# Three quarters of an expert's slots as lanes beside streamed weights, and GpSimd without the experts' low parts

## Chip, cores and metric

The kernel runs on one core of a Trainium2 chip. The metric is the device time of one execution in microseconds; a kernel's time is the median of its runs.

## What is computed

A trunk of two layers runs over 256 tokens (and 16 prepended ones). Each layer has a gated linear recurrence and a convolution, then a channel mixer. The second layer's mixer is a mixture of eight experts, and almost half of the time is spent on it:

```python
def moe_swiglu(x, w_router, w_gate, w_up, w_down):
    t = x.reshape(B * L, D)
    logits = (t @ w_router).astype(jnp.float32)
    top_val, top_idx = lax.top_k(logits, TOP_K)          # 2 of 8
    top_w = jax.nn.softmax(top_val, axis=-1)
    ...
    for e in range(N_EXPERTS):
        out = out + gates[:, e:e + 1] * swiglu(t, w_gate[e], w_up[e], w_down[e])
```

`swiglu(x)` is `(silu(x @ w_gate) * (x @ w_up)) @ w_down`. A token has 1024 channels, an expert 3584 hidden columns, and all of it is float32.

## The kernel before

**Precision.** TensorE takes float32 in a rounded form (float32r), so each float32 operand is split into a high part and a low part. A product is then three products: high by high, low by high, high by low. ScalarE (ACT) copies the high part of a piece of weights (`whi`, line 116), and another engine subtracts it from the raw piece to get the low part (`wlo`): VectorE (DVE, line 94) for most pieces, GpSimd (POOL, line 218) for those that `lo_pool` (line 315) names. Of the experts' 672 pieces, those with `i % 4 == 1` are GpSimd's, but for the last ones.

**Weights.** A piece is 1024 floats on each of 128 partitions (512 KB). SyncE's queue loads it (`load_ahead`, line 269, DMA issue on line 279) as soon as one of six `raw` buffers is free; a buffer is free when the low part has been made from it. Six `whi` and six `wlo` buffers hold split pieces, and a split buffer is free when TensorE has used it. `prep` (line 282) splits pieces in order, up to five ahead of the products. All engines work through their instructions in the order in which the program recorded them.

**Experts.** Tokens are gathered to slots by products with a one-hot matrix. The experts are sorted by their numbers of tokens into positions, except for position 0, which is fixed. Positions 0, 2 and 3 are *narrow*: 128 slots. Positions 4 to 7 are *slim*: 64 slots, where the array holds the 64 slots' high parts and their low parts side by side as 128 columns, so that two products (by `whi`, by `wlo`) give everything; `fold_parts` (line 576) adds the two halves with small products against a folding matrix. Position 1, the expert with the most tokens, is *wide*: 256 slots.

An *item* is gate, up or down for 512 of the hidden columns of one position; it takes four pieces of weights. Narrow and slim items hold the tokens in the array and stream 512 columns of weights past them: 24 products of 512 columns for a narrow item, 16 for a slim one. The wide gate and up items are turned round: the array holds 128x128 of the weights, and 256 slots stream past (lines 1497 to 1499), 96 products of 256 columns for an item. A wide down item has 48 products of 512 columns (lines 1481 to 1483), two tiles of 128 slots by three products.

**Order.** `moe_seq` (line 1337) makes positions 0, 2, 3 first (21 groups of gate, up, down), then positions 4, 5, 6 with one item of position 1 after each of their 21 groups (`WIDE`, line 53), then position 7 alone. A *round* below is one slim group and one wide item, 16 pieces. What evacuates a product is put on a list (`pend`, `pend2`) and recorded while the next item is under way: for a wide up item that is `times` (line 1544), which multiplies silu(gate) by up for 1024 floats and splits the result; for slim items `fold_parts`; for wide down items `gain` (line 1520), which adds a group's result to a sum.

**Overflow.** Tokens beyond a position's slots are handled after the main sequence, in a branch (`moe_rest`, line 1735) that runs only if there are any.

Of the kernel before, what the change touches and what calls it, by code (L numbers as in the profile page):

```python
# [42 lines left out]
# The product after which a block's evacuation comes; pieces to be ready after pairs of rows; the order of the  # L43
# parts (of the weights, of x) where several blocks are made at once.
# [4 lines left out]
# Experts by position: the first one is fixed, the others are sorted. Wide items after each group, the items before  # L49
# which a gather begins, the groups by which the last position's down products wait.  # L50
# [6 lines left out]
# Columns at which the engines share the rows of tokens, and products that keep the tensor engine's clock up.  # L57
# [11 lines left out]
class Halves:  # L69
    """A [128, 8, n] tensor kept as two tiles of four blocks."""  # L70
# [9 lines left out]
class Priced:  # L80
    """The vector engine, with an estimate of how long it has been given work for."""
# [17 lines left out]
class Tables:  # L99
    """The scalar engine; the functions are taken from three table sets."""  # L100
# [18 lines left out]
class Trunk:  # L119
# [101 lines left out]
    def plan(self):  # L221
# [3 lines left out]
        def piece(w, a, b, c0):  # L225
            """Up to four blocks of rows of a unit's columns."""
# [129 lines left out]
    def gemm_both(self, x, n, evacs, other, before=None):  # L356
        """Two units against all of n tokens, block of rows by block of rows, as x comes."""
# [34 lines left out]
    def level_bits(self):  # L392
        """The bits in which s and t differ, of t after s."""
# [95 lines left out]
    def rstd_col(self, mv, k):  # L489
        """mv[:, 1] holds a variance; returns 1 / sqrt(var + eps)."""  # L490
# [6 lines left out]
    def tok_mean(self, t, k, between=None):  # L497
        """[mean, variance] of the rows of t."""
# [23 lines left out]
    def input_norm(self, first):  # L522
        """The normalised tokens, transposed: returns their two parts and the work that makes a block."""
# [22 lines left out]
        def block(b):  # L546
            """The low part of a block waits until the next block is under way."""
# [17 lines left out]
    def norm_sums(self, s, r, first, eng=None):  # L565
        """Add a block to the sums of r and of r * r over the blocks."""
# [16 lines left out]
    def rstd(self, mu, e2, n):  # L583
        """1 / sqrt(e2 - mu * mu + eps)."""
# [16 lines left out]
    def post_norm(self, r, s, g, b):  # L601
        """h = LN(r) * g + b, in two float32r parts; the sums in s have all blocks but the last."""
# [45 lines left out]
    def residual(self, r, h, i):  # L648
        """r block i = ALPHA * h."""
# [3 lines left out]
    def add_to(self, r, ps, b, s):  # L653
        """A block of products added to r, and its part in the sums."""
# [51 lines left out]
    def forget(self, l, j, f, k):  # L706
        """f = lb + (1 - lb) sigmoid(z) and k = (1 - lb) sigmoid(-z); lb is zero in the first layer."""
# [11 lines left out]
    def values(self, i, ps, j):  # L719
        """The value projection of a head, copied out; its transposes come a block later."""  # L720
# [20 lines left out]
    def attention(self, hf, f, k, q):  # L741
        """Attention weights of four heads: att[s, t] = sum_d q[t] f[s + 1] ... f[t] k[s], s <= t.
        A level joins neighbouring runs of h tokens: q has the decay from its run's start, k the decay to its
        run's end, and the last of a run's f is the decay of the whole run. A mask keeps the pairs of tokens
        that a level is for; that of runs of one takes a token with itself along."""
# [47 lines left out]
        def join(h):  # L793
            """Runs of h tokens become runs of 2 h."""
# [64 lines left out]
    def heads(self, l, sog, o, t0, n):  # L859
        """o = RMS norm of att^T v per head, times the gate (the norm's gain is in it)."""  # L860
# [194 lines left out]
    def spread_rows(self, *names):  # L1055
        """Rows of parameters, put on all partitions by products."""
# [16 lines left out]
    def router_weights(self):  # L1073
        """LN(r) @ W = rstd * (r @ (g W) - mean * sum(g W)) + sum(b W), sums over d: g W and the two sums."""
# [17 lines left out]
    def residual_tok(self, h, res):  # L1092
        """ALPHA * h of the last 256 tokens, tokens on the partitions."""
# [12 lines left out]
    def out_proj1(self, mx, res):  # L1106
        """r = res + mx @ w_out with tokens on the partitions, LN(r), and the router's logits, which are taken
# [766 lines left out]
```

## Time and profile before

| | |
|---|---|
| time, median of 3 runs | 2014.54 us (2013.33 to 2029.12) |
| span of the profiled execution | 2016.8 us |
| busy in it: PE, PEld | 95%, 85% |
| busy in it: DVE, ACT, POOL | 78%, 62%, 46% |
| read from HBM | 481.73 MB, 239 GB/s over the span |

The profiled execution is 2.3 us above the median. Shares over the whole span mix stages with different limits, so the tables below are cut into stretches: the first two layers up to about 930 us, then the experts. An idle engine costs nothing unless the engine that sets the pace waits for it. Busy time of PE is modelled, and consecutive products overlap, so a product's cost is read from the distance between the starts of two, not from its duration.

### The profile page before, as it was taken

To read this page: it belongs to the slowest core of one execution; us is meant where nothing else is said; L and a number is where in the kernel's file an instruction comes from. 1 tells how busy PE (TensorE), PEld (TensorE's weight loads), DVE (VectorE), ACT (ScalarE), POOL (GpSimd) and SP (SyncE) were. 2 spreads that over 40 slices of the span, in tenths; PEclk is the share of its full clock that TensorE was granted. 3 is DMA by queue.
4 is the path that set the end of the run, shared out by engine and by line. 5 is a ranking of instruction groups with operands and counts; after the bars stand their busy time and mean duration, and the time that the engine had idled before them with its cause. 6 is when DMAs were issued, how large, how long until landed. Compare 5 with 4: busy or idle time off the path is not lost. (4 is left out here: it accounts for less than half of the span.)

```text
span 2016.8 us, 33666 instructions
## 1 busy us (share of the span) xinstructions
PE 1911.1 (95%) x12193; PEld 1719.1 (85%) x12193; DVE 1571.7 (78%) x1931; ACT 1256.5 (62%) x1707; POOL 930.5 (46%) x424
## 2 busy tenths in 40 slices
PE   9999998999999998998999999999999999999896
PEld 8999898999999998997778888887888887877664
DVE  7998628755568985378999888878878788788887
ACT  5445454544465444645767787777776766766775
POOL 6776756200078567624444444434443433434343
PEclk9999999999999999998999999999999999999998
DMA  6634344565555343564998999998998888999896
GB/s 199 186 116 136 116 128 135 158 176 166 171 157 166 115 126 115 157 204 156 353 335 299 351 358 350 355 334 304 324 317 311 311 312 304 323 316 316 296 344 221
DMA packets 284182, 485.08 MB, mean 241 GB/s; under 512 B 15042, under 2 KB 139842, under 8 KB 284006
## 3 DMA queue, kind: packets, MB, share of 16 engines
q1 hardware_dynamic: 283654, 481.75, 70.7%
q8 instruction: 97, 1.59, 0.3%
q0 software_dynamic: 320, 1.08, 0.1%
q14 instruction: 79, 0.65, 0.1%
q10 hardware_dynamic: 32, 0.01, 0.0%
HBM read 481.73 MB, written 1.05 MB: 239 GB/s over the span
## 5 line engine op out<-in xcount | busy, mean ns | idle before, releaser
L218 POOL TENSOR_TENSOR wlo<-raw,whi 128x1024 fp32r<-128x1024 f32 (+1 forms) x339 | 865.5, 2562 | 1011.4 <-ACT whi L116 970.4
L116 ACT ACTIVATE whi<-raw 128x1024 fp32r<-128x1024 f32 (+1 forms) x919 | 950.4, 1051 | 292.9 <-DMA raw<-in_moe_w_gate_dram 53.6
L94 DVE TENSOR_TENSOR wlo<-raw,whi 128x1024 fp32r<-128x1024 f32 (+1 forms) x578 | 829.9, 1476 | 192.4 <-ACT whi L116 188.1
L343 PE MATMUL mm<-h_hi,whi 128*128 128x272 f32 (+1 forms) x1280 | 378.5, 296 | 1.0 <-ACT tmp L116 1.0
L345 PE MATMUL mm<-h_hi,wlo 128*128 128x272 f32 (+1 forms) x1280 | 371.4, 290 | 0.0
L344 PE MATMUL mm<-h_lo,whi 128*128 128x272 f32 (+1 forms) x1280 | 370.1, 289 | 0.0
L343 PEld LDWEIGHTS mm<-h_hi,whi 128*128 128x128 f32 x1280 | 244.8, 191 | 2.6 <-ACT tmp L116 1.2
L344 PEld LDWEIGHTS mm<-h_lo,whi 128*128 128x128 f32 x1280 | 244.9, 191 | 0.1
L345 PEld LDWEIGHTS mm<-h_hi,wlo 128*128 128x128 f32 x1280 | 244.4, 191 | 0.0
L94 DVE SCALAR_TENSOR_TENSOR st<-wide,cw,st 128x272 f32<-128x272 f32 (+1 forms) x480 | 194.4, 487 | 0.0
L1490 PE MATMUL mm<-wlo,xg 128*128 128x512 f32 x448 | 180.3, 403 | 6.1 <-DVE wlo L94 3.9
L1489 PE MATMUL mm<-whi,xg 128*128 128x512 f32 x448 | 179.0, 400 | 0.0
L1503 PE MATMUL mm<-wlo,xg 128*128 128x512 f32 x336 | 131.8, 392 | 1.4 <-DVE wlo L94 1.3
L1501 PE MATMUL mm<-whi,xg 128*128 128x512 f32 x336 | 132.4, 394 | 0.0
L1502 PE MATMUL mm<-whi,xg 128*128 128x512 f32 x336 | 131.5, 391 | 0.0
L1497 PE MATMUL mm<-xg,whi 128*128 128x256 f32 x448 | 127.6, 285 | 0.0
L1499 PE MATMUL mm<-xg,wlo 128*128 128x256 f32 x448 | 126.8, 283 | 0.0
L1498 PE MATMUL mm<-xg,whi 128*128 128x256 f32 x448 | 126.7, 283 | 0.0
L1477 PE MATMUL st<-wlo,tmp 128*128 128x512 f32 x224 | 96.2, 429 | 22.8 <-DVE wlo L94 11.5
L1490 PEld LDWEIGHTS mm<-wlo,xg 128*128 128x128 f32 x448 | 86.0, 192 | 32.6 <-DVE wlo L94 11.3
L1489 PEld LDWEIGHTS mm<-whi,xg 128*128 128x128 f32 x448 | 86.2, 192 | 19.1 <-issue 0.8
L1476 PE MATMUL st<-whi,tmp 128*128 128x512 f32 x224 | 91.0, 406 | 1.6 <-DVE tmp L94 1.6
(368 smaller groups left out, 3461.8 us busy)
## 6 DMA issues: line engine op xcount, KB each, us to landing
raw<-in_moe_w_gate_dram SPq DMA_DIRECT2D x224, 512.0 KB, 5.2
raw<-in_moe_w_up_dram SPq DMA_DIRECT2D x224, 512.0 KB, 5.8
raw<-in_moe_w_down_dram SPq DMA_DIRECT2D x224, 512.0 KB, 5.1
raw<-in_w_in_dram SPq DMA_DIRECT2D x128, 512.0 KB, 3.8
raw<-in_ffn_w_gate_dram SPq DMA_DIRECT2D x22, 512.0 KB, 4.0
raw<-in_ffn_w_up_dram SPq DMA_DIRECT2D x22, 512.0 KB, 3.9
raw<-in_ffn_w_down_dram SPq DMA_DIRECT2D x20, 512.0 KB, 3.6
raw<-in_w_conv_out_dram SPq DMA_DIRECT2D x16, 512.0 KB, 3.4
```

Source lines behind the costliest of these rows:

```text
L94: return f(out, *a, **k)
L116: return self.eng.activation(out, in_, func, **k)
L218: (eng or self.V).tensor_tensor(lo, src, f32(hi), op=ALU.subtract)
L343: nc.tensor.matmul(ps[c], w[i][0][:, a], xh, start=first, stop=False)
L344: nc.tensor.matmul(ps[c], w[i][0][:, a], xl, start=False, stop=False)
L345: nc.tensor.matmul(ps[c], w[i][1][:, a], xh, start=False, stop=last)
L1489: nc.tensor.matmul(banks[0], x(2 * h + i), whi, start=first, stop=False)
L1490: nc.tensor.matmul(banks[0], x(2 * h + i), wlo, start=False, stop=last)
L1497: nc.tensor.matmul(dst, whi[:, cc], a, start=first, stop=False, skip_group_check=True)
L1501: nc.tensor.matmul(banks[0], a, whi, start=first, stop=False)
L1502: nc.tensor.matmul(banks[0], b, whi, start=False, stop=False)
L1503: nc.tensor.matmul(banks[0], a, wlo, start=False, stop=last)
```

## The change

Position 1 gets 192 slots in place of 256, as two lanes that stand in the array at the same time as separate stationary operands: 128 slots as a narrow position has them, and 64 more as a slim position has them (`SECOND`). All its items then stream 512 columns of weights past the slots, as other positions' items do: for each block of weights three products by `whi` (narrow lane high, narrow lane low, slim lane) and two by `wlo`. A wide item becomes 40 products of 512 columns. The narrow lane's hidden values are transposed on TensorE as for narrow positions, the slim lane's are folded as for slim ones. Position 1 gets its own overflow branch for tokens beyond 192. And `lo_pool` names only two of the experts' pieces, so VectorE makes the low parts of the other 166 that GpSimd made.

```diff
+FULL, SECOND = CAP + SLIM, "second"
...
     def lo_pool(self, i):
         if i >= DENSE:
-            return DENSE + 4 <= i < DENSE + 6 or i % 4 == 1 and i < PIECES - 4
+            return DENSE + 4 <= i < DENSE + 6
...
-        for j, (p, cap) in enumerate(((0, CAP), (2, CAP), (4, SLIM))):
+        for j, (p, cap) in enumerate(((0, CAP), (1, FULL), (2, CAP), (4, SLIM))):
...
     def moe_item(self, kind, p, g, wide, slim):
+        lanes = [(p, False), (SECOND, True)] if wide else [(p, slim)]
...
+                for i, (whi, wlo) in enumerate([(whi, wlo), *more]):
+                    high, low = [], []
+                    for (q, thin), d in zip(lanes, banks):
+                        x, k = self.x[q][0], 2 * h + i
+                        high += [(d, x(k))] if thin else [(d, x[0](k)), (d, x[1](k))]
+                        low += [(d, x(k) if thin else x[0](k))]
+                    self.products(high, low, whi, wlo, h == 0 and i == 0, h == 3 and i == 1)
-                        if wide:
-                            dst = banks[j // 2][:, (j % 2) * CW:(j % 2 + 1) * CW]
-                            cc = slice(j * P, (j + 1) * P)
-                            first = first and j % 2 == 0
-                            nc.tensor.matmul(dst, whi[:, cc], a, start=first, stop=False, skip_group_check=True)
-                            nc.tensor.matmul(dst, whi[:, cc], b, start=False, stop=False, skip_group_check=True)
-                            nc.tensor.matmul(dst, wlo[:, cc], a, start=False, stop=last, skip_group_check=True)
...
+        for (q, thin), d in zip(lanes, banks):
+            if thin:
+                self.pend.append(lambda q=q, d=d: self.fold_parts(kind, q, g, d))
+            elif kind == "g":
+                self.pend.append(lambda q=q, d=d: self.silu(q, g, d))
+            else:
+                self.pend.append(lambda q=q, d=d: self.times(q, g, d))
...
-                           GW: lambda: self.gather([1], self.key, 2 * CAP),
+                           GW: lambda: self.gather_lanes(1, self.key),
```

On TensorE, the end of the first wide up item and the start of the slim item behind it. In the kernel before, `xg` are the 256 slots, streamed past 128 columns of `whi` and `wlo`:

```order
L1497 MATMUL mm_14588<-xg_13336,whi_14564 128x256
L1498 MATMUL mm_14588<-xg_13338,whi_14564 128x256
L1499 MATMUL mm_14588<-xg_13336,wlo_14565 128x256
L1489 MATMUL mm_14716<-whi_14574,xg_12344 128x512
L1490 MATMUL mm_14716<-wlo_14575,xg_12344 128x512
```

With the change, `xg_13338` and `xg_13339` are the narrow lane's high and low parts and `xg_13340` is the slim lane:

```order
L1553 MATMUL mm_14541<-whi_14518,xg_13338 128x512
L1553 MATMUL mm_14541<-whi_14518,xg_13339 128x512
L1553 MATMUL mm_14542<-whi_14518,xg_13340 128x512
L1556 MATMUL mm_14541<-wlo_14519,xg_13338 128x512
L1556 MATMUL mm_14542<-wlo_14519,xg_13340 128x512
L1553 MATMUL mm_14614<-whi_14528,xg_12345 128x512
L1556 MATMUL mm_14614<-wlo_14529,xg_12345 128x512
```

Three rows that stood four times for a block of weights have become five rows that stand once. Behind the slim item, where the kernel before had no row of position 1, the change has the narrow lane's transposes and the slim lane's folding products:

```order
L1553 MATMUL mm_14614<-whi_14594,xg_12700 128x512
L1556 MATMUL mm_14614<-wlo_14595,xg_12700 128x512
L1601 MATMUL ca_14659<-ident,four_14629 128x128 x4
L1625 MATMUL ca_14664<-fold,four_14400 128x64 x4
L1625 MATMUL ca_14664<-fold,four_14629 128x64 x4
L1553 MATMUL mm_14673<-whi_14610,xg_12345 128x512
L1556 MATMUL mm_14673<-wlo_14611,xg_12345 128x512
```

These twelve small products are new on TensorE, and they wait for `four_14629`, which VectorE writes. On VectorE, the same place of the kernel before; the first two rows are a slim position's, the `four` and `fw` rows are the wide position's `times`:

```order
L1596 TENSOR_TENSOR tmp_14644<-tmp_14643,ca_14578 128x256
L94 TENSOR_TENSOR tmp_14645<-tmp_14644,tmp_14645 128x4x64
L94 TENSOR_TENSOR wlo_14653<-raw_14524,whi_14652 128x1024
L94 TENSOR_TENSOR wlo_14683<-raw_14539,whi_14682 128x1024
L94 TENSOR_TENSOR wlo_14713<-raw_14552,whi_14712 128x1024
L1549 TENSOR_TENSOR four_14731<-four_14446,mm_14587 128x512
L1549 TENSOR_TENSOR four_14731<-four_14446,mm_14588 128x512
L94 TENSOR_TENSOR wlo_14739<-raw_14572,whi_14738 128x1024
L94 TENSOR_TENSOR wlo_14749<-raw_14613,whi_14748 128x1024
L94 TENSOR_TENSOR wlo_14759<-raw_14650,whi_14758 128x1024
L94 TENSOR_TENSOR fw_14735<-four_14731,fw_14734 128x1024
```

and with the change:

```order
L97 TENSOR_TENSOR wlo_14622<-raw_14516,whi_14621 128x1024
L1594 TENSOR_TENSOR four_14629<-four_14400,mm_14541 128x512
L97 TENSOR_TENSOR wlo_14636<-raw_14526,whi_14635 128x1024
L97 TENSOR_TENSOR wlo_14646<-raw_14553,whi_14645 128x1024
L97 TENSOR_TENSOR wlo_14656<-raw_14576,whi_14655 128x1024
L97 TENSOR_TENSOR wlo_14681<-raw_14592,whi_14680 128x1024
L97 TENSOR_TENSOR fs_14631<-ca_14659,fs_14631 128x512
L1631 TENSOR_TENSOR tmp_14693<-tmp_14692,ca_14664 128x256
L97 TENSOR_TENSOR fs_14694<-tmp_14693,fs_14694 128x4x64
L97 TENSOR_TENSOR wlo_14702<-raw_14608,whi_14701 128x1024
```

Four `wlo` rows stand where three stood, and the products of 1024 floats of the wide position (two `L1549` rows and the `fw` row) have become one product of 512, one split of 512 read from PSUM, and the slim lane's two rows of 256.

## Rows read from the trace of the kernel before

**Rows 1.** The page, its first line.

```profile
span 2016.8 us, 33666 instructions
```

**Rows 2.** Stretches: us, busy PE, PEld, DVE, ACT, POOL, granted clock, DMA share, GB/s.

```profile
941.00:1056.00 115.00, 108.40 (x488) 85.60 (x487) 113.68 (x92) 82.51 (x92) 52.83 (x18) 1.00 0.88 313
1056.00:1103.00 47.00, 47.00 (x214) 38.81 (x214) 42.70 (x36) 38.31 (x43) 22.59 (x8) 1.00 0.82 294
1103.00:1304.00 201.00, 200.72 (x938) 166.76 (x937) 170.07 (x144) 157.59 (x170) 85.97 (x34) 1.00 0.98 353
1310.00:1872.00 562.00, 532.23 (x3060) 460.15 (x3060) 459.60 (x360) 394.26 (x458) 225.25 (x84) 0.98 0.90 315
1872.00:1999.00 127.00, 112.81 (x485) 80.02 (x483) 109.03 (x94) 97.96 (x121) 50.85 (x19) 0.97 0.90 319
```

**Rows 3.** Timeline of PE: start, duration, then the instruction; two wide, then slim products.

```profile
1401.04 0.28 PE L1498 MATMUL mm<-xg,whi 128*128 128x256 f32 x1
1401.16 0.28 PE L1499 MATMUL mm<-xg,wlo 128*128 128x256 f32 x1
...
1419.36 0.39 PE L1476 MATMUL st<-whi,tmp 128*128 128x512 f32 x1
1419.59 0.39 PE L1477 MATMUL st<-wlo,tmp 128*128 128x512 f32 x1
...
1424.44 1.89 PE L1590 MATMUL ca<-fold,tmp 128*128 128x64 f32 x16
1426.14 0.36 PE L1497 MATMUL mm<-xg,whi 128*128 128x256 f32 x1
```

**Rows 4.** Waits in 1310:1872: us in total, times, longest.

```profile
PEld st L1477 <- DVE wlo L94: 19.8, 23, 2.2
...
PEld st L1477 <- POOL wlo L218: 13.3, 11, 1.5
```

**Rows 5.** Waits of the DMA queue in 1310:1872.

```profile
SPq L279 <- POOL wlo L218: 166.0, 73, 3.6
```

**Rows 6.** VectorE's durations in 1310:1872, ns, least/median/most.

```profile
L94 DVE TENSOR_TENSOR wlo<-raw,whi x252: 1207/1212/3420, 1309.2 to 1866.4; 128x1024 fp32r<-128x1024 f32 x126
...
L94 DVE TENSOR_TENSOR tmp<-tmp,tmp x21: 424/1560/1742, 1334.8 to 1857.3; 128x256 fp32r<-128x256 f32 x21
```

**Rows 7.** Timelines of DVE (two rows) and POOL (two rows), one place.

```profile
1399.85 3.68 DVE L94 TENSOR_TENSOR wlo<-raw,whi 128x1024 fp32r<-128x1024 f32 x2 [0.78 <-ACT whi L116]
...
1408.81 3.48 DVE L94 TENSOR_TENSOR wlo<-raw,whi 128x1024 fp32r<-128x1024 f32 x3
...
1398.46 2.84 POOL L218 TENSOR_TENSOR wlo<-raw,whi 128x1024 fp32r<-128x1024 f32 x1 [2.75 <-ACT whi L116]
...
1413.35 2.41 POOL L218 TENSOR_TENSOR wlo<-raw,whi 128x1024 fp32r<-128x1024 f32 x1 [4.74 <-ACT whi L116]
```

**Rows 8.** Groups in 1310:1872: busy us, mean ns | idle before.

```profile
L94 DVE TENSOR_TENSOR wlo<-raw,whi 128x1024 fp32r<-128x1024 f32 x252 | 367.7, 1504 | 83.4 <-ACT whi L116 80.2 <-PE st L1476 1.9 <-PE mm L1499 0.7
...
L218 POOL TENSOR_TENSOR wlo<-raw,whi 128x1024 fp32r<-128x1024 f32 x84 | 225.2, 2682 | 337.2 <-ACT whi L116 315.4 <-PE mm L1489 7.6 <-PE mm L1498 4.8
...
L94 DVE TENSOR_TENSOR tmp<-tmp,tmp 128x256 fp32r<-128x256 f32 x21 | 27.4, 1304 | 10.2 <-ACT tmp L116 10.2
...
L94 DVE TENSOR_TENSOR fw<-four,fw 128x1024 fp32r<-128x1024 f32 x7 | 21.7, 3093 | 0.0
...
L1549 DVE TENSOR_TENSOR four<-four,mm 128x512 f32<-128x512 f32 x14 | 9.5, 682 | 0.3
```

**Rows 9.** The low parts' groups in 941:1056 (two rows), 1103:1304 and 1872:1999.

```profile
L94 DVE TENSOR_TENSOR wlo<-raw,whi 128x1024 fp32r<-128x1024 f32 x55 | 99.6, 1863 | 1.1 <-ACT whi L116 1.1
...
L218 POOL TENSOR_TENSOR wlo<-raw,whi 128x1024 fp32r<-128x1024 f32 x18 | 52.8, 2935 | 60.8 <-ACT whi L116 60.8
...
L94 DVE TENSOR_TENSOR wlo<-raw,whi 128x1024 fp32r<-128x1024 f32 x102 | 142.1, 1433 | 25.6 <-ACT whi L116 24.8
...
L94 DVE TENSOR_TENSOR wlo<-raw,whi 128x1024 fp32r<-128x1024 f32 x62 | 87.4, 1456 | 11.1 <-ACT whi L116 11.0
```

More of the change, by code (lines that the diff above doesn't have):

```diff
@@ L1450, in gather, with gather_lanes, tiles, slice_ @@
             self.tasks += todo
+    def gather_lanes(self, p, key):
+        nc = self.nc
+        xs, box = {}, {"left": KB}
+        def tiles():
+            box["oh"] = self.one_hot([p], key, 2 * CAP)
+            for part in (0, 1, SECOND):
+                xs[part] = self.hs.tile([P, KB, P], F32R, tag="hs", name=self.name("xg"))
+        def slice_(kk, part):
+            def f():
+                src, oh = self.parts[part], box["oh"]
+                pt = self.ca((P, 2, 2 * CAP))
+                for i in range(2):
+                    k = 2 * kk + i
+                    for tt in range(2):
+                        nc.tensor.matmul(pt[:, i], src[tt][:, k * P:(k + 1) * P], oh[:, tt, 0], start=tt == 0, stop=tt == 1)
+                def evac():
+                    box["left"] -= 1
+                    b = slice(2 * kk, 2 * kk + 2)
+                    a = slice(part * SLIM, (part + 1) * SLIM)
+                    for dst, v in ((xs[part][:, b], pt[:, :, :CAP]), (xs[SECOND][:, b, a], pt[:, :, CAP:FULL])):
+                        if part:
+                            self.A.activation(dst, v, AF.Copy)
+                        else:
+                            nc.vector.tensor_copy(dst, v)
+                self.pend.append(evac)
+            return f
+        self.x[p] = [[lambda k, part=part: xs[part][:, k, :] for part in range(2)], box, 0]
+        self.x[SECOND] = [lambda k: xs[SECOND][:, k, :], box, 0]
+        self.tasks += [tiles] + [slice_(kk, part) for part in range(2) for kk in range(4)]
     def moe_item(self, kind, p, g, wide, slim):
         nc = self.nc
+        lanes = [(p, False), (SECOND, True)] if wide else [(p, slim)]
         if kind == "d" and wide:
@@ L1458, in moe_item @@
             self.y[p] = [[self.st((P, 512)) for _ in range(2)]]
-        while kind == "d" and (p, g) not in self.hid:
+        while kind == "d" and any((q, g) not in self.hid for q, _ in lanes):
             self.flush()
@@ new lines, in moe_item @@
+                first, last = h == 0 and (wide or g == 0), h == 3 and (wide or g == G - 1)
+                for c in range(2):
+                    cc = slice(c * 512, (c + 1) * 512)
+                    high, low = [], []
+                    for (_, thin), y, f in zip(lanes, self.y[p], hid):
+                        high += [(y[c], f[:, h])] if thin else [(y[c], f[0][:, h]), (y[c], f[1][:, h])]
+                        low += [(y[c], f[:, h] if thin else f[0][:, h])]
+                    self.products(high, low, whi[:, cc], wlo[:, cc], first, last)
+            else:
+                for i, (whi, wlo) in enumerate([(whi, wlo), *more]):
+                    high, low = [], []
+                    for (q, thin), d in zip(lanes, banks):
[3 more added lines that the diff above has]
+                    self.products(high, low, whi, wlo, h == 0 and i == 0, h == 3 and i == 1)
@@ L1508, in moe_item, with products @@
             self.prep(self.used + SPLIT - 1)
-        if slim and kind != "d":
-            self.pend.append(lambda: self.fold_parts(kind, p, g, banks[0]))
-        elif kind == "g":
-            self.pend.append(lambda: self.silu(p, g, banks))
-        elif kind == "u":
-            self.pend.append(lambda: self.times(p, g, banks, wide))
-        elif wide:
-            self.pend.append(lambda: self.gain(p, g, self.y[p]))
-        elif g == G - 1:
-            self.pend.append(lambda: self.finish(p))
+        if kind == "d":
+            if wide:
+                self.pend.append(lambda: self.gain(p, g, self.y[p]))
+            elif g == G - 1:
+                self.pend.append(lambda: self.finish(p))
+            return
+        for (q, thin), d in zip(lanes, banks):
[3 more added lines that the diff above has]
+                self.pend.append(lambda q=q, d=d: self.silu(q, g, d))
+            else:
+                self.pend.append(lambda q=q, d=d: self.times(q, g, d))
+    def products(self, high, low, whi, wlo, first, last):
+        seen = []
+        for d, x in high:
+            self.nc.tensor.matmul(d, x, whi, start=first and not any(d is e for e in seen), stop=False)
+            seen.append(d)
+        for d, x in low:
+            self.nc.tensor.matmul(d, x, wlo, start=False, stop=last)
     def gain(self, p, g, ys):
@@ L1533, in gain, with silu, lane_tmp @@
             self.finish(p)
-    def silu(self, p, g, banks):
-        t = self.four(F32) if len(banks) == 2 else self.tmp([P, 512])
-        for i, b in enumerate(banks):
-            self.A.activation(t[:, i * 512:(i + 1) * 512], b, AF.Silu)
+    def silu(self, p, g, bank):
+        t = self.lane_tmp(p)
+        self.A.activation(t, bank, AF.Silu)
         self.sg[p] = t
+    def lane_tmp(self, p):
+        if p == SECOND:
+            t, self.shared = self.shared, None
+            return t[:, 512:]
+        if not (p == 1 and self.lanes):
+            return self.tmp([P, 512])
+        self.shared = self.four(F32)
+        return self.shared[:, :512]
@@ L1541, in four, with times, turn @@
     def four(self, dt):
         return self.mp.tile([P, D], dt, tag="four", name=self.name("four"), bufs=6)
[L1544 removed]
+    def times(self, p, g, bank):
         nc = self.nc
[L1546 to L1550 removed]
+        f = self.lane_tmp(p)
+        nc.vector.tensor_tensor(f, self.sg[p], bank, op=ALU.mult)
+        fs = self.hs.tile([P, 2, 4, P], F32R, tag="hs", name=self.name("fs"))
+        fh, fl = fs[:, 0], fs[:, 1]
+        def turn():
+            pt = self.ca((P, 4, P))
+            for i in range(4):
+                nc.tensor.transpose(pt[:, i, :], f[:, i * P:(i + 1) * P], self.ident)
@@ L1673, in moe_run @@
     def moe_run(self, seq, start, ahead=0, wide=(), slim=()):
+        self.lanes = bool(wide)
         for n, (kind, p, g) in enumerate(seq):
@@ L1746, in moe_rest @@
                     for p in ps:
-                        self.y_hs = p > 2
+                        self.y_hs = p not in (0, 2)
                         n = nc.values_load(self.count[0:1, p:p + 1], min_val=0, max_val=S)
```

81 lines of the change are left out of this document (19 added, 62 removed).

## The prediction

> **What bounds the kernel now.** I read the stretches first [rows 2]. Up to 930 us the change touches nothing; all terms lie behind. The first narrow items (941 to 1056) have VectorE busy 113.68 of 115 us: VectorE is the limit there, while the transfers run at 313 GB/s. The short stretch to 1103 has PE busy throughout, with a gather among its products. The next 201 us run at 353 GB/s with a DMA share of 0.98: the weights' transfer is the limit. From 1310 to 1872, the 21 rounds of slim and wide items, no engine is full: DMA share 0.90, PE 532 of 562, VectorE 460. A round takes 562 / 21 = 26.76 us. Position 7 alone (1872 to 1999) is at 0.90 of DMA again.
>
> Why no engine is full in the rounds is read from the timeline of PE [rows 3]. A product of 256 columns starts 0.12 us after the one before, one of 512 columns 0.23 us. So a slim group is 48 x 0.23 = 11.04 us, its folding 1.70 (1424.44 to 1426.14). A wide gate or up item is 96 x 0.12 = 11.52, a wide down item 48 x 0.23 = 11.04, 11.36 in the mean. Together 24.10 us, so 2.66 us of a round is lost. The waits say where: slim down products wait for low parts, of VectorE 19.8 us and of GpSimd 13.3 us [rows 4]. The loads run behind too: the DMA queue waited 166.0 us for raw buffers that GpSimd's subtraction still held, though most of that was spent with other loads in flight [rows 5]. At 353 GB/s [rows 2] a piece of 0.524 MB costs 1.485 us, sixteen 23.8 us. So PE's own work, 24.10, is the largest floor of a round, and buffers that come late add the rest.
>
> **The lanes.** A wide item becomes 40 products of 512 columns: 40 x 0.23 = 9.20 us in place of 11.36. The pitch should hold: every product loads its stationary operand anew already now, 3060 loads for 3060 products [rows 2]. For three items the slim lane adds one folding (1.70 us) and the narrow lane four transposes. A folding product of 64 columns is 1.70 / 16 = 0.11 us; the four transposes have 128, so between as much and twice as much each, 0.4 to 0.9 us; I take 0.9. PE's round is then 12.74 + (27.6 + 2.6) / 3 = 22.8 us, 1.3 less. On VectorE, seven times, two products of 512 floats (0.682 each [rows 8]) and a split of 1024 (3.093) give way to one product and one split of 512 (I take 0.682 for both) and the slim lane's two rows of 256 floats, 0.424 each where undisturbed [rows 6]. ACT gets a copy, a silu and a split of the slim lane more; at 394 of 562 us [rows 2], even as much for each of the seven groups as VectorE's longest split here, 3.1 us, leaves it at 19.8 us a round. The gather keeps its products and one more copy of 64 slots hides behind PE in the narrow stretch.
>
> **The low parts.** VectorE makes 166 more pieces. What one costs is not the mean of now. In the rounds the mean is 1504 ns [rows 8], but least and median are 1207 and 1212, the longest 3420 [rows 6]. The timelines show which is which [rows 7]: two pieces at 1399.85 took 3.68 us while GpSimd's piece of 1398.46 ran until 1401.30; three at 1408.81 took 3.48, in GpSimd's idle stretch before 1413.35. GpSimd's subtraction of 2682 ns [rows 8] pushes VectorE's aside. Without it I take 1.212 for each. Bounds: 1.16 (3.48 / 3) and the mean of now, 1.504. So in the rounds VectorE's work is 336 x 1.212 = 407, the slim splits 21 x 0.424 = 9, the wide position's 7 x 2.21 = 15.5, and what is left of now (459.6 - 367.7 - 27.4 - 21.7 - 9.5 = 33.3): 465 us, 22.1 a round. It hardly rises from 459.6, though it makes a third more pieces.
>
> The Trainium skill (Perfetto Trace Analysis, Optimizing Scalar/DVE Operations) says that when VectorE is saturated, giving work to ScalarE or even GpSimd may make sense. It adds that VectorE and GpSimd share a read port, so that moving work between those two might not help. The first sentence speaks against this change and would keep the 225 us on GpSimd; the trace sides with the second.
>
> **The sum.** In the rounds three floors lie close: transfers 23.8, PE 22.8, VectorE 22.1. A round cannot be under 23.8: 500 us, -62. If PE's loss of 2.66 stayed, it would be 25.5: 535 us, -27. GpSimd's share of the waits goes, but VectorE's queue is in order, and a multiply that waits for TensorE or ScalarE now holds up every low part. I take the middle, 24.6: 517 us, **-45**. In 941 to 1056, VectorE's 99.6 us for 55 pieces [rows 9] become (55 + 18) x 1.212 = 88.5, with the other 14.1 us 102.6; the bytes (313 GB/s x 115) need 102 at 353 GB/s. I take 105, **-10** (bounds 0 and -13). To 1103 PE stays full: 0. In 1103 to 1304 the transfers stay the limit; VectorE's work is 201 x 353 / 524 = 135 pieces x 1.212 = 164 and 170.07 - 142.1 [rows 2, 9] = 28 beside: 192 of 201, so 0, but 4 us later if its waits don't hide. In 1872 to 1999 there are 77 pieces: VectorE 93 + (109.03 - 87.4) = 115 us [rows 2, 9], transfers 115; I take **-3** (bounds 0 and -12). Together -58: 2016.8 [rows 1] becomes 1959. The profiled execution was 2.3 us above the median, so **1957**.
>
> **Rivals.** *The transfers alone decide.* If the buffers keep the queue fed, every stretch but the PE-bound one runs at 353 GB/s: -62 - 13 - 12 = -87, 1927. For it: the stretch at 0.98 shows it can be done with PE and VectorE busy. Against: in the rounds PE takes slim pieces every 0.92 us and wide ones every 2.3, with twelve buffers to even that out. The Trainium skill (Perfetto Trace Analysis, Engine Utilization) gives 358 GB/s as a core's full memory bandwidth; by that a round would be 23.4 us, an estimate, and the trace's 353 agrees.
> *The loss moves to VectorE's queue.* With all low parts in one queue, behind evacuations that wait for PE, the loss of a round grows from 2.66 to 4.0 and eats what PE saves: 26.8 again. Only the -10 at the start stays: 2005. For it: VectorE's lateness is already the larger wait [rows 4]. Against: its work per round stays where it was.
> *VectorE stays slow, and the kernel gets slower.* If the long subtractions have another cause than GpSimd (TensorE's reads or the transfers), a piece stays at 1.504. The rounds are then (336 x 1.504 + 58) / 21 = 26.8 before any wait, and with 1 us of waits 27.8: +22. The first narrow items need 73 x 1.504 + 14 = 124 (+9), those to 1304 135 x 1.433 + 28 = 221 (+20), position 7 77 x 1.456 + 22 = 134 (+7): +58, 2072. It decides from a price of about 1.44, where 336 pieces and the 58 us beside fill the rounds of now with 1 us of waits in each. Against it speaks [rows 7].
> *The lanes don't hold the tokens.* From 193 tokens at position 1 on, the branch runs an expert again, 84 pieces x 1.485 = 125 us. The reference's router on its inputs gives the largest expert 179, so hardly.
>
> **Chances.** My forecast 0.60 (1938 to 1985), transfers alone 0.20, loss moves 0.11, slower 0.08, overflow 0.01. The range runs from 1926, the transfers' case, to 1996; it leaves out the last three, 0.20. A measurement of this kernel tells about 1% from no change, 1994 to 2035: faster 0.80, same 0.11, slower 0.09.
>
> **What would show it.** In the profile after: products of a wide item 0.23 us apart; VectorE's low parts at 1.21 us with mean near median; GpSimd idle; the rounds' DMA share at 0.95 or more and PE's share down; 941 to 1056 shorter by 10 us, the stretch behind it unchanged. Waits of slim down products for GpSimd are gone; if those for VectorE more than double, the second rival has come. It would be wrong if wide products keep more than 0.25 us apart, or if longer waits of PE in the rounds bring its granted clock under the 0.98 of now.

## The result and the profile after

The changed kernel takes 1952.77 us, median of 5 runs (1951.73 to 1962.13). Against the kernel before, run on the same chip (median of its five runs there 2020.70 us, three of which are those of the table before), that is a ratio of 0.9673 with a 95% interval of 0.9642 to 0.9704. The forecast was 1957 in a range of 1926 to 1996.

The profiled execution of the changed kernel was the slowest of its five, 1962.13 us, so its span is compared with the span before, not with the median. The page's first line, and the stretches that answer to [rows 2] (columns as there; PE is TensorE): the narrow items in three pieces, the rounds, position 7. The first begins with the first product of the experts, some 50 products earlier than the one at 941 us of [rows 2], and the third ends with the last product of the narrow items, 28 products later than the one to 1304 us there, so their lengths are not to be set beside those rows:

```profile
span 1960.4 us, 32273 instructions
...
936.00:1054.00 118.00, 117.46 (x537) 97.21 (x537) 107.68 (x130) 93.05 (x102) 0.00 (x0) 0.99 0.92 338
1054.00:1101.00 47.00, 47.00 (x214) 38.81 (x214) 44.66 (x43) 37.83 (x43) 0.00 (x0) 1.00 0.83 289
1101.00:1308.00 207.00, 207.00 (x966) 172.22 (x965) 192.01 (x190) 163.52 (x180) 0.00 (x0) 1.00 0.98 356
1308.00:1816.00 508.00, 495.41 (x2354) 405.71 (x2354) 446.10 (x447) 393.47 (x474) 0.00 (x0) 0.99 0.97 346
1816.00:1942.00 126.00, 110.83 (x490) 82.08 (x488) 110.46 (x115) 98.60 (x124) 0.00 (x0) 0.97 0.92 327
```

The rounds take 508 us in place of 562, 24.2 us each in place of 26.76, at 346 GB/s and a DMA share of 0.97 in place of 0.90. That is most of the gain. VectorE's busy time in them is 446, less than the 460 of before, although it makes a third more low parts. PE's busy share of them rises, from 532 of 562 us to 495 of 508. Position 7 is 1 us shorter.

One profile is one execution. A kernel of the experiments below, the changed one with needless fills on GpSimd, was profiled in an execution of 1946 us; its rounds took 502 us and its position 7 took 122. So a few us of a difference between two profiles can be the execution's.

The narrow items from the first product of the experts to the first slim product, in the kernel before (first line) and in the changed one (second):

```profile
928.70:1310.00 381.30, 374.42 (x1713) 306.25 (x1714) 338.26 (x290) 291.70 (x317) 166.41 (x62) 1.00 0.92 331
```

```profile
936.00:1307.80 371.80, 371.26 (x1714) 308.07 (x1714) 344.15 (x361) 294.31 (x322) 0.00 (x0) 1.00 0.94 342
```

From 381.3 us they went to 371.8, 9.5 us less, and nearly all of it lies in front of the gather: the products up to the 1056 us of [rows 2] took 127.3 us before and take 118 now. The changed kernel arrives 7 us later at the first product; what runs up to there is the same in both programs but for the first few low parts, and the kernels of the experiments arrive between 931 and 936. The profile of before was the earliest of all and this one the latest.

VectorE's low parts in the rounds, least, median and most, which answers to [rows 6], and the first waits of slim down products, which answer to [rows 4]:

```profile
L97 DVE TENSOR_TENSOR wlo<-raw,whi x334: 1214/1221/1229, 1307.7 to 1813.3; 128x1024 fp32r<-128x1024 f32 x167
```

```profile
PEld st L1556 <- DVE wlo L97: 11.1, 27, 1.1
```

The spread is gone: all lie between 1214 and 1229 ns. TensorE's wait for VectorE fell from 19.8 to 11.1 us, the one for GpSimd is no longer there. The timeline of PE in a wide down item shows the new products' pitch (a start every 0.23 us):

```profile
1365.48 0.39 PE L1553 MATMUL mm<-whi,fs 128*128 128x512 f32 x1
1365.72 0.40 PE L1556 MATMUL ca<-wlo,fs 128*128 128x512 f32 x1
```

### The profile page after: what moved, and what is told of

Read it like the earlier page. It is cut to its first block, busy times and chain, and to the rows that moved or that the text cites. A ratio compares the mean times of both kernels' runs of the same rounds, so it can differ in the third digit from the quotient of the medians.

```text
span 1960.4 us, 32273 instructions
## 1 busy us (share of the span) xinstructions
PE 1869.9 (95%) x11493; PEld 1669.0 (85%) x11493; DVE 1575.6 (80%) x2111; ACT 1258.9 (64%) x1732; POOL 483.8 (25%) x258
## 5 line engine op out<-in xcount | busy, mean ns | idle before, releaser
L97 DVE TENSOR_TENSOR wlo<-raw,whi 128x1024 fp32r<-128x1024 f32 (+1 forms) x744 | 880.3, 1218 | 147.9 <-ACT whi L119 129.9
L221 POOL TENSOR_TENSOR wlo<-raw,whi 128x1024 fp32r<-128x1024 f32 (+1 forms) x173 | 418.7, 2438 | 374.6 <-ACT whi L119 361.1
L1556 PE MATMUL mm<-wlo,xg 128*128 128x512 f32 x1008 | 378.8, 394 | 4.2 <-DVE wlo L97 4.1
L348 PE MATMUL mm<-h_hi,wlo 128*128 128x272 f32 (+1 forms) x1280 | 371.8, 290 | 0.0
L1553 PEld LDWEIGHTS mm<-whi,xg 128*128 128x128 f32 x1456 | 273.4, 190 | 63.1 <-ACT whi L119 5.0
L1556 PEld LDWEIGHTS mm<-wlo,xg 128*128 128x128 f32 x1008 | 190.9, 189 | 49.6 <-DVE wlo L97 9.9
L1553 PE MATMUL st<-whi,fs 128*128 128x512 f32 x336 | 104.3, 391 | 0.5 <-DVE fs L97 0.5
L119 ACT ACTIVATE tmp<-mm 128x512 f32<-128x512 f32 (+1 forms) x115 | 59.4, 519 | 42.5 <-PE mm L348 42.3
L1553 PEld LDWEIGHTS st<-whi,fs 128*128 128x128 f32 x336 | 62.2, 188 | 13.3 <-DVE fs L97 1.0
L1556 PE MATMUL st<-wlo,fs 128*128 128x512 f32 x168 | 65.6, 391 | 0.0
L1556 PEld LDWEIGHTS st<-wlo,tmp 128*128 128x128 f32 x224 | 43.4, 194 | 24.9 <-DVE wlo L97 16.4
```

The costliest lines, as they stand in the source:

```text
L97: return f(out, *a, **k)
L119: return self.eng.activation(out, in_, func, **k)
L348: nc.tensor.matmul(ps[c], w[i][1][:, a], xh, start=False, stop=last)
L1553: self.nc.tensor.matmul(d, x, whi, start=first and not any(d is e for e in seen), stop=False)
L1556: self.nc.tensor.matmul(d, x, wlo, start=False, stop=last)
```

## The experiments

Each ratio is to the kernel before, run beside it on the same chip, with its 95% interval. The experiments ran on three chips, and the median of the kernel before went from 2016 to 2020 us between them, so a difference of a few us between two experiments on different chips shows nothing. At the end of the section a table puts the rounds of the kernels side by side.

### The two halves of the change, each alone

The lanes alone are the changed kernel with the old rule for GpSimd:

```diff
-            return DENSE + 4 <= i < DENSE + 6
+            return DENSE + 4 <= i < DENSE + 6 or i % 4 == 1 and i < PIECES - 4
```

> The lanes alone: GpSimd keeps the low parts it had. Theory (TensorE's own work was the largest floor of a round, and GpSimd's subtraction holds VectorE up): a low part of VectorE stays at a mean near 1.5 us and TensorE's loss of 2.7 us a round stays, so a round is 22.8 + 2.7 = 25.5 us, the rounds take 535, the first narrow items stay at 115, and the time is about 27 us under the kernel before, 1988 to 1995. Rival (the lanes carry it all): within 8 us of the changed kernel, about 1955. Rival (GpSimd carries it all): no different from the kernel before.

Measured: 1975.36 us, ratio 0.979 (0.9747 to 0.9834), 13 us under my range and 20 above the 1955 of the first rival.

The low parts alone are the kernel before with the new rule:

> The low parts alone: the wide position as before, VectorE makes the low parts that GpSimd made. Theory: VectorE's low parts fall to 1.21 us each and its work in a round is about 22.3 us, under TensorE's 24.1, which now sets the pace with less lost beside it: rounds of 25.3 us (531), the first narrow items 10 us shorter, about 35 to 40 us under the kernel before, 1975 to 1985. Rival (one queue for all low parts makes TensorE wait more): rounds of 26.8 or more, 2005 to 2030. Rival (the lanes carry it all): no different from the kernel before.

Measured: 1988.71 us, ratio 0.9858 (0.9821 to 0.9895), 4 us above my range. The rounds of both (first line the lanes alone, second the low parts alone):

```profile
1314.00:1829.70 515.70, 498.22 (x2359) 405.40 (x2358) 425.35 (x368) 399.60 (x478) 215.96 (x84) 0.99 0.97 342
```

```profile
1304.00:1846.00 542.00, 526.08 (x3060) 456.32 (x3059) 449.68 (x440) 388.39 (x453) 0.00 (x0) 0.99 0.93 326
```

The lanes alone give 46 of the 54 us that the rounds lost; the low parts alone give 20. So the parts overlap: either shortens the same loss. My number for the lanes alone, 25.5 us a round, was 0.9 too high: TensorE's loss did not stay at 2.7 but fell to 24.56 - 22.8 = 1.8, about as with the low parts alone (25.8 - 24.1 = 1.7, where I had 25.3 - 24.1 = 1.2). The narrow items are the low parts' alone: between the same two products as above they take 381.8 us with the lanes alone, as before, and 369.9 with the low parts alone.

```profile
932.10:1313.90 381.80, 375.34 (x1715) 306.79 (x1715) 337.54 (x297) 292.68 (x322) 166.48 (x62) 1.00 0.93 333
```

```profile
934.00:1303.90 369.90, 369.72 (x1714) 306.73 (x1714) 343.36 (x354) 294.27 (x319) 0.00 (x0) 1.00 0.96 344
```

One reading of mine falls here. In the rounds of the lanes alone VectorE is busy for 425 us, in those of the changed kernel for 446, and the changed kernel is the faster. So it is not VectorE's total work that GpSimd's share lengthened. What is left is lateness: a low part on GpSimd took about 2.6 us, and neither its split buffer nor its raw buffer moves on before that. The waits fit: with the lanes alone slim down products wait as long for VectorE as in the changed kernel (11.7 us against 11.1), and for GpSimd on top of it:

```profile
PEld st L1556 <- POOL wlo L221: 12.6, 11, 1.8
```

Single low parts of VectorE took up to 3.4 us there, too, and no run parts their lateness from that of GpSimd's own.

### What GpSimd does to VectorE

Two kernels give GpSimd work that nobody needs, behind the pieces whose low parts it made before. Nothing waits for it, so only what it does to others can change the time.

```diff
+            if i >= DENSE + 6 and i % 4 == 1 and i < PIECES - 4:
+                self.idle_work()
...
+    def idle_work(self):
+        for _ in range(4):
+            self.nc.gpsimd.tensor_tensor(self.dum, self.iota, self.iota, op=ALU.add)
...
```

> The changed kernel with work for GpSimd that nobody needs: behind each piece whose low part GpSimd made before, four additions of 256 floats, two operands from SBUF that are constants, the result read by nobody. No engine waits for it. Theory (GpSimd's subtraction holds VectorE's up while it reads SBUF): the mean of VectorE's low parts rises from 1.22 to between 1.4 and 1.6 us, and with some 22.1 us of work a round becoming 25 to 26, the time rises by 30 to 60 us, to 1985 to 2015. Rival (the long subtractions had come from waiting or from the raw buffers): mean 1.22, time 1953 within 0.5%.

Measured: 2078.76 us, ratio 1.0298 (1.0258 to 1.0338): slower, as the theory had it, but 64 us past the end of its range. The other has this in its place:

```diff
+        for _ in range(8):
+            self.nc.gpsimd.memset(self.dum, 0.0)
```

> As the kernel with needless additions, but GpSimd fills 256 floats eight times instead, about as long a time, which writes SBUF and reads nothing. Theory (reads of GpSimd are what holds VectorE up): mean of VectorE's low parts 1.22 us, time 1953 within 0.5%. Rival (any GpSimd work holds VectorE up): mean 1.4 to 1.6, time 1985 to 2015, as with the additions.

Measured: 1952.88 us, ratio 0.9687 (0.9643 to 0.9732), as the theory had it. VectorE's low parts with the additions, in the rounds, and with the fills, in the narrow stretch, where most of the fills ran (they wait for nothing and so ran ahead; third, GpSimd's own row there, and last, the rounds of this kernel):

```profile
L97 DVE TENSOR_TENSOR wlo<-raw,whi x334: 1207/1629/1662, 1359.7 to 1933.6; 128x1024 fp32r<-128x1024 f32 x167
```

```profile
L97 DVE TENSOR_TENSOR wlo<-raw,whi x250: 1211/1225/1228, 935.2 to 1301.4; 128x1024 fp32r<-128x1024 f32 x125
```

```profile
L316 POOL MEMSET dum<- 128x256 f32 x988 | 309.3, 313 | 56.8
```

```profile
1302.00:1804.00 502.00, 491.35 (x2357) 403.98 (x2356) 445.51 (x448) 393.43 (x475) 99.64 (x319) 1.00 0.98 351
```

With GpSimd busy for 309 of 366 us by writing alone, no low part of VectorE was over 1228 ns. With additions, which read and write, the median is 1629. So what made the long ones of before is not that GpSimd was busy, nor its writing, but its instructions that read SBUF. The Trainium skill (SBUF — State Buffer, Who interferes with whom) says that a VectorE instruction with two SBUF inputs contends with a GpSimd instruction that reads SBUF, not with one that only writes it; the trace agrees, with 1629 against 1225 ns.

The 126 us of the additions are no price for the change, though. They ran one behind the other and took twice the time of the subtractions that they stand for:

```profile
L316 POOL TENSOR_TENSOR dum<-iota 128x256 f32<-128x256 f32 x364 | 468.7, 1288 | 28.5
```

468.7 us for the 364 of the rounds, against 225.2 for the subtractions of before [rows 8], and VectorE had all 16 low parts of a round to make as well. What the kernel does show is that the third rival of the prediction had a possible case: with low parts at a mean of 1534 ns the rounds took 577 us, where that rival had 584 (27.8 x 21). That the whole time lies near its 2072 is luck: against the kernel before, the narrow items lost 44 us where it had 29, and position 7, where no additions were left, lost none of its 7.

### How much of GpSimd is too much

```diff
-            return DENSE + 4 <= i < DENSE + 6
+            return DENSE + 4 <= i < DENSE + 6 or i % 8 == 1 and i < PIECES - 4
```

> The changed kernel with every eighth of the experts' low parts on GpSimd, half of what it had before the change. With a quarter of them there the time was 22 us longer than with none. Theory (each low part on GpSimd costs the others about as much: it is late itself and holds VectorE up): 1960 to 1967. Rival (a few are taken without harm, and relieve VectorE): 1945 to 1955.

Measured: 1968.42 us, ratio 0.9742 (0.9703 to 0.9781), 1 us above the theory's range and 16 us more than with none. A quarter of the low parts costs 23 us, an eighth 16. The two intervals overlap, so the 7 us between them are not sure; but the eighth's interval, from 0.9703, begins where the changed kernel's ends, so a small share isn't free.

### TensorE's columns, up and down

One product more for each block of weights of a wide item, so that it has 48 products of 512 columns again, in the new form:

```diff
-        for d, x in high:
+        for d, x in high + (high[-1:] if len(low) > 1 else []):
```

> The changed kernel with one more product for each block of weights of a wide item (the slim lane by the high part, a second time, which is added to the sums): 48 products of 512 columns as in the kernel before, in the changed form. TensorE's round is 22.8 + 8 x 0.23 = 24.6 us. Theory (it is the number of columns that the lanes save, and TensorE then passes the transfers as the largest floor): rounds of 25.5 to 26.3, as with the low parts alone, so 1980 to 1995. Rival (it is the form, fewer and longer products, that helps): 1953 to 1962.

Measured: 1977.35 us, ratio 0.9816 (0.9764 to 0.9867), 25 us above the changed kernel and 3 under the theory's range. So the columns count: 1.84 us more work made a round 25.3 us, 1.1 longer than in the profile of the changed kernel and 1.4 longer than in that with the fills. But the form may have a share of its own. This kernel and the one with the low parts alone stream the same number of columns in a wide item and differ in the form alone; here PE's work is the larger (24.6 against 24.1, for the folding and the transposes) and the round still the shorter (25.3 against 25.8). That is 11 us over the rounds, and the times differ by as much, 1977.35 against 1988.71; but the two intervals overlap, so it isn't sure. The other way, without the slim lane:

```diff
-        lanes = [(p, False), (SECOND, True)] if wide else [(p, slim)]
+        lanes = [(p, False)] if wide else [(p, slim)]
...
```

> The changed kernel without the slim lane: position 1's tokens beyond 128 are left out, a wide item is 24 products of 512 columns and has no folding. TensorE's work in a round falls from 22.8 to about 18.5 us, the transfers stay at 23.8. Theory (with the change the transfers set the pace of the rounds): rounds of 24.2 us go to no less than 23.7, the time falls by at most 10 us, 1942 to 1953. Rival (TensorE still sets the pace): rounds of 20 to 21, 1870 to 1890.

Measured: 1928.06 us, ratio 0.9551 (0.9501 to 0.9601). Neither theory nor rival: 25 us less, where I had allowed 10 or asked for 65 and more. The rounds show a part of why:

```profile
1306.00:1789.00 483.00, 436.03 (x1908) 326.60 (x1907) 433.52 (x419) 383.38 (x443) 0.00 (x0) 0.98 1.00 362
```

PE has 47 us to spare here, and a round still takes 23.0. The rate is 362 GB/s, 0.524 MB / 362 = 1.448 us a piece and 23.2 a round, so 23.8 was no floor. I had taken it from a stretch at 353 GB/s and a share of 0.98 in which PE was busy for 200.72 of 201 us [rows 2]: PE was at its limit there, and the transfers kept up. A DMA share of 1.00 isn't the transfers' limit either. Among the narrow items of the changed kernel, with PE busy throughout, there is a stretch of 49 us at 384:

```profile
980.00:1029.00 49.00, 49.00 (x229) 40.73 (x228) 46.81 (x49) 38.59 (x41) 0.00 (x0) 1.00 1.03 384
```

At that rate a round's transfers would need 21.8 us. What holds the rounds at 23.0 without the slim lane is open: the transfers, as my theory had it, or the six raw buffers, for which the DMA queue waited 269 us in these rounds, too.

### VectorE's queue

Without the 166 low parts that GpSimd made before (the high part stands in):

```diff
+            if i >= DENSE + 6 and i % 4 == 1 and i < PIECES - 4:
+                self.A.activation(hi, t, AF.Copy)
+                self.ready.append([hi.rearrange("p (k n) -> p k n", k=k)] * 2)
+                continue
```

> The changed kernel without the low parts that GpSimd made before: for those 166 pieces the high part stands in for the low one, so products and transfers stay and VectorE has 12 low parts a round in place of 16, about 17 us of work in place of 22. Theory (transfers set the pace, VectorE's queue costs less than 0.5 us a round): the time falls by at most 15 us, 1938 to 1953, the DMA share of the rounds goes from 0.97 to 0.98 or more. Rival (VectorE's queue sets the pace): rounds under 23.5 us cannot be, since the transfers forbid it, but position 7 and the narrow items get shorter too, together more than 15 us, under 1938.

Measured: 1937.01 us, ratio 0.9608 (0.956 to 0.9655), 16 us less, on the border of theory and rival. In the rounds:

```profile
1304.00:1797.00 493.00, 485.40 (x2360) 404.66 (x2360) 358.01 (x369) 399.10 (x479) 0.00 (x0) 1.00 0.99 358
```

VectorE's work falls by 88 us and the rounds by 15, or by 9 from the 502 us of the kernel with the fills. So it isn't VectorE's total that sets the pace, but its queue costs the rounds 0.4 to 0.7 us each; whether that is more than the 0.5 that I had written down isn't shown. Nor is it the queue's time alone: the raw buffer of a piece without a low part is free as soon as ScalarE has copied it.

### What is left to gain

Two more raw buffers for the slim positions' pieces, from buffers that the narrow positions no longer use:

```diff
+MORE = 510, 900, 2
...
-            n, room = i, {False: RAW, True: EXTRA}
+            n, room = i, {False: RAW, True: EXTRA if i < END else MORE[2]}
...
-        return AHEAD <= i < END and (i - AHEAD) % (RAW + EXTRA) < EXTRA
+        return AHEAD <= i < END and (i - AHEAD) % (RAW + EXTRA) < EXTRA or MORE[0] <= i < MORE[1] and i % (RAW + MORE[2]) < MORE[2]
```

They were first tried together with a thinner spread of the wide items, which also moves two small steps of position 7 (the spreading of two vectors over the partitions and an early turn) to later items:

```diff
-WIDE = [0] * 21 + [1] * 21
+WIDE = [0] * 21 + [1, 1, 1, 1, 0, 1, 1] * 3 + [1, 1, 1, 0, 0, 0, 0]
...
-                           (7, 1): lambda: self.spread_rows("ln2_g", "ln2_b"),
-                           (7, 4): lambda: self.turn_ahead(7)}, 2, [1], slim)
+                           (7, 4): lambda: self.spread_rows("ln2_g", "ln2_b"),
+                           (7, 5): lambda: self.turn_ahead(7)}, 2, [1], slim)
```

> The changed kernel with two attempts at the rest: the wide items are spread thinner (18 after the groups of positions 4 to 6, three after those of position 7), and two more buffers for raw pieces from the sixth hundred of pieces on, eight in place of six. If the transfers set the pace and late buffers cost them the last 3% of the rounds and 8% in position 7, the time falls by 5 to 15 us, 1938 to 1948. If the losses have other causes, 1950 to 1956.

Measured: 1940.54 us, ratio 0.9623 (0.9576 to 0.9669). Then each alone, and both with ten buffers:

> The changed kernel with the wide items spread thinner alone (18 after groups of positions 4 to 6, three after those of position 7), six raw buffers as before. If the thinner rounds, in which TensorE has 22.0 us in place of 22.8, gave the 12 us of the kernel with both attempts: 1938 to 1945. If the two more buffers gave them: 1949 to 1956.

Measured: 1959.74 us, ratio 0.97 (0.966 to 0.9741), above both ranges.

> The changed kernel with eight raw buffers in place of six from the sixth hundred of pieces on, alone. If late raw buffers are what keeps the rounds' DMA share at 0.97 and position 7's at 0.92: 1938 to 1945, with the rounds at 0.99. If the thinner spread gave the 12 us: 1949 to 1956.

Measured: **1932.14 us, ratio 0.9562 (0.9528 to 0.9597)**, 6 us under the range. Its rounds, and the DMA queue's first wait in them; below it the same wait in the rounds of the changed kernel:

```profile
1304.00:1793.80 489.80, 486.11 (x2359) 403.31 (x2358) 440.02 (x448) 384.41 (x475) 0.00 (x0) 1.00 0.99 362
```

```profile
SPq L283 <- DVE wlo L98: 271.2, 232, 6.9
```

```profile
SPq L282 <- DVE wlo L97: 290.8, 316, 4.9
```

> Both attempts with ten raw buffers in place of eight. If buffers still hold transfers back: 1930 to 1937. If the rounds are at the transfers' own rate (362 to 365 GB/s at share 1.00, as without the slim lane) and only position 7 and the tail are left: 1937 to 1942.

Measured: 1941.69 us, ratio 0.9612 (0.9578 to 0.9646).

The buffers gave all of it. The thinner spread costs some 8 us with them; the 7 without them are not sure, since the interval overlaps that of the changed kernel. Ten buffers are no better than eight, with the thinner spread, with which alone they were tried. With eight the rounds run at 362 GB/s with all of the computation in them, and this version is 21 us faster than the changed kernel. The queue waits for raw buffers nearly as long in total as with six, so the total of that wait doesn't tell what it costs. PE is busy for 486.11 of 489.80 us there, so that PE, and not the transfers, may set the pace again. Why the thinner spread costs, and whether the wide items or the two moved steps do it, is open: its last stretch (1780 to 1940 us), where three wide items stand among position 7's, runs at 321 GB/s.

The rounds of all kernels but those with the thinner spread, each from one profile and from stretches like those above; PE's work is the sum of products at their pitch, worked out as in the prediction:

| kernel | PE's work in a round | a round | over PE's work | GB/s, DMA share |
|---|---|---|---|---|
| before | 24.1 | 26.8 | 2.7 | 315, 0.90 |
| low parts alone | 24.1 | 25.8 | 1.7 | 326, 0.93 |
| lanes alone | 22.8 | 24.6 | 1.8 | 342, 0.97 |
| changed | 22.8 | 24.2 | 1.4 | 346, 0.97 |
| changed, needless fills | 22.8 | 23.9 | 1.1 | 351, 0.98 |
| changed, needless additions | 22.8 | 27.5 | 4.7 | 305, 0.90 |
| changed, an eighth of low parts on GpSimd | 22.8 | 24.7 | 1.9 | 340, 0.96 |
| changed, one more product | 24.6 | 25.3 | 0.7 | 332, 0.94 |
| changed, a quarter of low parts left out | 22.8 | 23.5 | 0.7 | 358, 0.99 |
| changed, eight raw buffers | 22.8 | 23.3 | 0.5 | 362, 0.99 |
| changed, no slim lane | 18.6 | 23.0 | 4.4 | 362, 1.00 |

The row of the one more product was 531 us of rounds, from 1305 to 1836:

```profile
1305.00:1836.00 531.00, 525.13 (x2526) 434.65 (x2525) 446.42 (x448) 392.21 (x475) 0.00 (x0) 1.00 0.94 332
```

## Why the prediction came out as it did

**What bounds the rounds: right for the kernel before, not for the changed one.** PE's own work was the largest floor, and a round was that plus late buffers. The columns taken away and put back (the slim lane left out, one more product) move the time the way that needs, and the pitch of 0.23 us held. But the sum made the transfers the floor of the new rounds, with PE's share down as a sign. PE's share went up, from 0.95 to 0.98, and two more raw buffers, which change neither PE's work nor the bytes, took 0.6 to 0.9 us more out of a round, so the rounds still look like PE's work plus late buffers. The other signs came, and PE's granted clock in the rounds was 0.99, not under 0.98.

**The price of a low part: right in its cause, a little high in its sum.** 1.212 us was taken, 1.222 is the mean in the whole stretch of the experts, and the kernels with needless work for GpSimd show the cause that the argument named. VectorE's busy time in the rounds was put at 465 us and was 446. Most of the 19 us lies in adding up durations: low parts one behind the other overlap, so 334 of them kept VectorE busy for 393.4 us, 1.18 each (first number behind the bar), near the 1.16 that the prediction had only as a bound. The sum had 407.

```profile
L97 DVE TENSOR_TENSOR wlo<-raw,whi 128x1024 fp32r<-128x1024 f32 x334 | 393.4, 1222 | 48.1 <-ACT whi L119 42.9
```

**The rounds: -45 expected, -54 measured (-60 in the kernel with the fills).** Two terms were mis-sized. "A round cannot be under 23.8": the floor of the transfers is 23.2 or less, by the 362 GB/s of the kernel without the slim lane and of the one with eight buffers; the 353 that I took was a rate at which PE was full, and the rounds of 23.0 and 23.3 us lie under the second estimate, 23.4, as well. And "if PE's loss of 2.66 stayed" as the case for lanes without the rest: it fell to 1.8 with the lanes alone. The middle of two bounds that both lay too high gave 24.6, the chip 24.2. Why the loss falls with the lanes is open; the kernel with one more product has a loss of 0.7 without shorter wide items, where the low parts alone have 1.7, so it may come with the form.

**The narrow items: -10 expected, about -9.5 measured.** VectorE's and the transfers' needs were weighed, 102.6 and 102 us, and PE's was left out. PE is busy for 117.46 of 118 us there after the change, and for all of the next two stretches: it was the next limit, right behind VectorE, and its 108.40 us of busy time stood in the row of before [rows 2]. The margin of 2.4 us that made 105 of 102.6 had no reason of its own; that it left room for PE was luck.

**Position 7 and 1103 to 1304: -3 and 0 expected.** Position 7 gave 1 in the profile of the changed kernel and 5 in that with the fills; the stretch of the narrow items behind the gather kept its pace (353 GB/s before, 356 after).

**Rivals.** The transfers alone (1927) had the rate too low and every stretch at it, which no kernel shows; the kernel with eight buffers nearly has its time, 1932, with rounds under its 23.8 us. It shows that the changed kernel's six don't keep the queue fed. The loss did not move to VectorE's queue: TensorE's waits for it fell, and the DMA queue's waits for low parts went from 356 us (190 for VectorE, 166 for GpSimd) to 291, all for VectorE. The queue isn't free, though, as the kernel without a quarter of the low parts shows. Getting slower needed low parts at 1.44 us or more, and they cost 1.22. The branch for tokens beyond 192 slots did not run: no expert's pieces follow position 7's.

**The total.** -58 was expected of the profiled span and -56 came, but 7 us were lost before the experts, where the change does nothing. From the first product of the experts on, 1088 us became 1024, which is -64: more than forecast, by the 9 us of the rounds, and position 7 takes 2 of them back. That the two spans differ by nearly what was forecast is luck, of two executions. The medians tell the same as the experts: 62 us less than the three runs of before, 68 less than the five.

## What to carry to other kernels

Before a transfer rate is used as a floor, look whether another engine was full in the stretch that it is read from: a rate that was reached is what the transfers can do at least, not at most, and a DMA share near 1.00 doesn't change that. An engine that helps out with a slower instruction can cost more by being late than it saves the other one in work, even when the other one's busy time goes down: judge it by the waits on its results and on the buffers that it holds. And when three engines' needs lie within 10% of each other, two more buffers can give as much as a redistribution of the work: here 21 us, as many as the low parts gave on top of the lanes (23). Last, one profile is one execution: set the same stretch of two or three kernels side by side before some us are called a gain.

## What was not expected of the hardware

The weights' stream reached 362 GB/s over 480 us at a DMA share of 0.99 to 1.00, and 384 over 49 us at 1.03, while the stretch with a share of 0.98 before the change showed 353. GpSimd's fills cost VectorE nothing even when GpSimd was busy for 85% of a stretch. And its additions of 256 floats, two reads each, took 1288 ns in the mean beside a busy VectorE, where the subtraction of 1024 floats had taken 2682: about twice as much for each element. The quickest of the additions took 611 ns, so their shortness alone doesn't make it; how it splits between contention and the instruction itself no run shows.
